# Spacing the recurrence tasks of a hybrid pooling and recurrence block

## The chip, the cores and the metric

The kernel runs on one core of a Trainium2 chip. The metric is the device time of one execution in microseconds (us); the kernel before takes 2507.37 us in the median of three runs (2506.67 to 2508.52).

## The reference

One layer on a sequence of 2048 positions with 1024 channels, all in float32:

- `xn = rmsnorm(x)`; one input projection `z = xn @ w_in` gives pooling channels, and for a gated recurrence of 4 heads of width 128 the queries `q`, forget logits `f`, values and output gate; also two branch gates of 1024 channels.
- Branch A: trailing-window means (windows 2, 4, 8, 16, one for each group of 128 channels) minus the token, a small matrix for each group, then `w_pa`.
- Branch B: for each head a state `S` of 128 x 128, `S_t = diag(f_t) S_(t-1) + (1 - f_t) v_t`, output `q_t S_t`, normalized, gated, then `w_pb`.
- The branches are merged with the gates, projected with `w_o` and added to `x`.
- Then a feed-forward block: up-projection to 2 x 2816, a causal convolution of width 3, a gated product, down-projection, and a last normalization.

## The kernel before, in words

TensorE does all matrix products. Each weight and each activation is split into a high and a low part, and a product is three matmuls for each 128 rows of depth. The large products use a scheme with seven block products in place of eight (P1 to P7), with the sums and differences of blocks made beforehand by VectorE, ScalarE, Pool and DMAs.

The sequence is worked in two halves of 1024 positions. Each half goes through `mixer` and then `ffn`. A mixer first computes values and output gate (`io`) and stores them in memory (`vd`, `zd`). It then runs 14 **units** in the order of the table `PROJ` (L55): `fq` h is the projection for head h, `g` the branch gates, `u` the pooling channels. A unit is seven products of 12 matmuls, for both blocks of 512 positions of the half. In the first mixer a unit also makes sums of weights and stores them for the second, and eight units are each followed by a small product of weights (`both`, L967, tiles `cw`). After the units come the products `pa` (branch A), `pb` (branch B) and `wo`.

Side work runs as Python generators (**tasks**) that are advanced while the instructions are written down: every 6 main matmuls (`MM_PER_TICK`, L79) there is a **tick**, and a task that yields n goes on n ticks later. So ticks set where a side instruction stands in its engine's queue among the main ones. Each engine works through its queue in order.

- `hgrn_task` (L996) is the recurrence of one head for one block of 512 positions: loads of values (L1002), then levels of doubling width, each with small matmuls into `pl` (L1059, L1105, L1118), masked copies into `at` on VectorE (L1073, L1112, L1125) and multiplications of `q`, `k` and `f`; then the transpose `pk` (L1139), the product `pv` with the values (L1148), the state chain `ss` on VectorE (L1156), the output `po` (L1164, L1166), its gating `ot` (L1177) and the transpose back `pt` (L1183). The task of a head's second block waits, before `pv`, until the first block's has written its `po`.
- When an `fq` unit ends, two such tasks (both blocks of one head) are put in `queue` (L1454). Three runners (L1426, L1434) each take one when they are free.
- `pool_task` (L944) makes the window sums of one group, on Pool for even groups and on VectorE for odd ones, from the results of a `u` unit; the second `u` unit has groups 2 and 3. The result is spilled to memory (`md`).
- `pa_task` (L1498) starts in the last unit: it loads the pooled blocks (`mx`) on SyncE's queue and makes the forms that `pa` multiplies. `o_task` (L1636) loads the heads' results and splits them from place 17 on (`O_PLACE`, L70; a place is one product of the last unit or of `pa`).

SyncE issues most loads in one queue: weights (`raw`), `v`, `z`, `mx`. All 512-wide work tiles come from one pool of 77 (`N_SLOTS`, L60), and the eight PSUM banks from another.

Of the kernel before, what the change touches and what calls it, by code (L numbers as in the profile page):

```python
# [51 lines left out]
FORM = {"P1": "B11", "P2": "B21", "P3": "B22", "P4": "T4", "P5": "T1", "P6": "T2", "P7": "T3"}  # L52
FIRST = ("P1", "P6", "P5")
BANK = {"P1": "X", "P2": "X", "P6": "Z", "P7": "Z", "P4": "Z", "P5": "V", "P3": "V"}
PROJ = (("fq", 0), ("g", 0), ("u", 0), ("fq", 1), ("g", 1), ("g", 2), ("fq", 2), ("g", 3),  # L55
        ("u", 1), ("g", 4), ("fq", 3), ("g", 5), ("g", 6), ("g", 7))

M_ORDER = (0, 4, 1, 5, 2, 6, 3, 7)

# [7 lines left out]
GO_IO = (("P2", 1), ("P2", 0))  # L67
G_POOL = 4
CW_AT = 2
O_PLACE = 17  # L70
FIN_WAIT = 4
AHEAD = 3
# [6 lines left out]
MM_PER_TICK = 6  # L79
# [3 lines left out]
def tile_trunk(  # L83
# [26 lines left out]
    def slot(name, cols=TB, dt=F32):  # L110
        return slots.tile([P, cols], dt, tag="s", name=name, padded_shape=[P, 528])

    def bank(name, cols=512):
        return banks.tile([P, cols], F32, tag="b", name=name, padded_shape=[P, 512])
# [6 lines left out]
    count = [0, None]  # L121
# [167 lines left out]
    def in_turn(ins):  # L289

        tc.add_manual_dep(ins.ins, count[1].ins.name, mybir.DependencyInfo(
            mybir.DependencyClass.NoSync, mybir.DependencyReason.SCHED_ONLY), reason="in turn")
        return ins
# [72 lines left out]
    def plan_io(b0):  # L366
        sevens = {}
        for p in IO_ORDER:
            for k in range(4):

                q = [w_io[k, :, c * 512 : (c + 1) * 512] for c in (0, 3, 1, 2)]
                one = {"P1": 0, "P2": 1, "P4": 3}
                if p in one:
                    plan_one("io", q[one[p]])
                    continue
                if b0:
                    plan_one("io", lambda k=k, p=p: kept["io", k, p])
                    continue
                if p == "P5":
                    if not k:  # L380
                        for i in range(4):
                            r0, r2 = (w_io[i, :, c * 512 : (c + 1) * 512] for c in (0, 1))
                            sevens[i] = stream.raw(r2, r0)
                    plan_one("io", lambda k=k: kept.get(("io", k, "P5")))
                    continue
                if p == "P6":
                    raws = [stream.raw(q[i]) for i in (2, 3, 0)]
                elif p == "P7":
                    raws = [sevens[k]]
                else:  # L390
                    raws = [stream.raw(lambda k=k: kept.get(("io", k, "P6")), q[1])]

                def fn(nm, k=k, p=p, raws=raws):
                    if p != "P6":
                        keep(("io", k, p), raws[0].tile, True)
                        return raws[0].tile
                    t = raws[0].tile
                    for i, r in enumerate(raws[1:]):
                        t2 = slot(f"{nm}s{i}")
                        dve.tensor_tensor(t2, t, r.tile, ALU.add)  # L400
                        t = t2
                        keep(("io", k, "P6" if i else "P5"), t)
                    return t

                stream.op("io", fn, raws)

    def plan_unit(key, src, kind, i, order, b0):
        mv, mg = proj_tiles(kind, i)
        if b0:
            unit = sums_of_unit(src, mv, mg, lambda p: lambda: kept["in", (kind, i), SUM_OF[p]])  # L410
        else:
            unit = weights_of_unit(quarters(src[mv], src[mg]), (kind, i))
        for p in order:
            fn, raws = unit[p]()
            stream.op(key, fn, raws)

    def plan_mixer(b0):
        plan_io(b0)
        for n, (kind, i) in enumerate(PROJ):
            if not b0 and (kind, i) == ("u", 0):  # L420
                r = stream.raw(pool_wt)
                stream.op("pw", None, [r])
            plan_unit("in", w_in_t, kind, i, ORDER, b0)
            if not b0 and 0 <= n - CW_AT < 8:
                g, c = divmod(n - CW_AT, 2)
                r = stream.raw(w_pa[g][:, c * 512 : c * 512 + 512])
# [569 lines left out]
    def hgrn_task(b, h, d, q, vd, zd, od):  # L996
        def head_of(src, key):
            t = slot(f"{key}{b}_{h}")
            sp.dma_start(t.rearrange("p (c v) -> p c v", c=NT), src[:, :, h * P : (h + 1) * P])
            return t  # L1000

        vt = head_of(vd, "v")  # L1002
        ks = slot(f"k{b}_{h}")
        act.activation(d, d, AF.Identity, bias=lbt[:, 2, h : h + 1], scale=lbt[:, 3, h : h + 1])
        act.activation(ks, d, AF.Identity, bias=1.0, scale=-1.0)
# [14 lines left out]
        def mask(key, n):  # L1020
            m = masks[key]
            return m.unsqueeze(1).to_broadcast([P, n, m.shape[1], m.shape[2]])
# [67 lines left out]
        for lv in (0, 1, 2, 4, 6):  # L1090
            hh = 1 << lv
            if lv in (2, 4):
                yield from two_levels(hh)
                continue
            nb = P // (2 * hh)
            qv = q.rearrange("p (c b t h) -> p c b t h", c=NT, t=2, h=hh)
            av = att.rearrange("p (c b t h) -> p c b t h", c=NT, t=2, h=hh)
            if lv < 2:
                qd, ad = ((q1, ae), (q2, ao))[lv]
                if lv == 1:  # L1100
                    act.copy(q2[:, :, 0].rearrange("p c (b h) -> p c b h", h=2), qv[:, :, :, 1, :])
                    yield AHEAD
                pa_ = bank(f"pl{b}_{h}_{hh}")
                for c in range(NT):
                    ins = pe.matmul(pa_[:, c * P : (c + 1) * P], ks[:, c * P : (c + 1) * P],  # L1105
                                    qd[:, c].rearrange("p s x -> p (s x)"),
                                    start=True, stop=True)
                    if not c:
                        in_turn(ins)
                yield 2  # L1110
                pv4 = pa_.rearrange("p (c s x) -> p c s x", c=NT, s=2)
                dve.copy_predicated(ad, masks[-1 - lv].to_broadcast([P, NT, 64]), pv4[:, :, 1])  # L1112
                pv4 = pv4[:, :, 0].rearrange("p c (b h) -> p c b h", h=hh)
            else:
                yield AHEAD
                pa_ = bank(f"pl{b}_{h}_{hh}", 256)
                for c in range(NT):
                    ins = pe.matmul(pa_[:hh, c * hh : (c + 1) * hh], ks[:, c * P : c * P + hh],  # L1118
                                    qv[:, c, 0, 1, :], start=True, stop=True)
                    if not c:  # L1120
                        in_turn(ins)
                yield 2
                act.copy(av[:hh, :, 0, 1, :], pa_[:hh].rearrange("p (c h) -> p c h", c=NT))
            if lv < 2:
                dve.copy_predicated(av[:, :, :, 1, :], mask(hh, NT), pv4)  # L1125
            q3 = q.rearrange("p (b t h) -> p b t h", t=2, h=hh)
            k3 = ks.rearrange("p (b t h) -> p b t h", t=2, h=hh)
            d3 = d.rearrange("p (b t h) -> p b t h", t=2, h=hh)
            full = [P, NT * nb, hh]
            if lv:  # L1130
                dve.tensor_tensor(q3[:, :, 1, :], q3[:, :, 1, :],
                                  d3[:, :, 0, 0:1].to_broadcast(full), ALU.mult)
            dve.tensor_tensor(k3[:, :, 0, :], k3[:, :, 0, :],
                              d3[:, :, 1, 0:1].to_broadcast(full), ALU.mult)
            dve.tensor_tensor(d3[:, :, 0, 0:1], d3[:, :, 0, 0:1], d3[:, :, 1, 0:1], ALU.mult)
        yield 4
        pk = bank(f"pk{b}_{h}")
        for c in range(NT):
# [270 lines left out]
    def mixer(b0, forms, late):  # L1409
        vd = [dram.tile([P, NT, 512], F32, tag=f"vd{b0}_{hf}", name=f"vd{b0}_{hf}")  # L1410
              for hf in range(2)]
# [9 lines left out]


        queue = []
        taken = [0]

        def runner():  # L1426
            while taken[0] < 2 * HEADS:
                if queue:
                    taken[0] += 1
                    yield from hgrn_task(*queue.pop(0))  # L1430
                else:
                    yield 1

        runners = [Task(runner()) for _ in range(N_RUN)]  # L1434
        fq = {}
# [121 lines left out]
        oT = {}  # L1557
        for n, (kind, i) in enumerate(PROJ):
            if not b0 and (kind, i) == ("u", 0):
                held["w"] = stream.get("pw")  # L1560
            u = Unit(f"{kind[0]}r{b0}_{i}", "in", emits[kind](i))
            for p in ORDER:
                u.multiply(p, forms, late)
                u.after(p)
                if n == len(PROJ) - 1:
                    if p == "P1":
                        quiet[0] = True
                        mtask = Task(pa_task())
                    place[0] += 1
            if not b0 and 0 <= n - CW_AT < 8:  # L1570
                both(n - CW_AT, held["w"])
                if n - CW_AT == 7:
                    stream.used(1)
# [62 lines left out]
        def o_task():  # L1636
            t = {}
            for hf in range(2):
                for g in range(HEADS):
                    while (b0 + hf, g) not in od:  # L1640
                        yield 1
                    t[hf, g] = fetch(od[b0 + hf, g], f"oT{b0 + hf}_{g}")
            while place[0] < O_PLACE:
                yield 1
# [363 lines left out]
```

## Time and profile before

| | us |
|---|---|
| median of three runs | 2507.37 |
| profiled execution, device time | 2510.01 |
| its span, first to last instruction | 2508.3 |
| TensorE busy | 2480.1 |
| VectorE busy | 2010.1 |
| ScalarE busy | 1200.3 |
| Pool busy | 816.2 |

A busy TensorE isn't always TensorE at its peak, since the ends of matmuls are modelled. PE in the rows is TensorE, PEld its weight load, DVE is VectorE, ACT ScalarE, POOL Pool, SP SyncE; a q behind a name is that engine's own queue. `L1073` is line 1073 of the kernel before.

### The profile page before, as it was taken

Reading aid. Unit: us, or ns where it says so; the run is one execution under the profiler, and the core shown is the slowest. Engines: PE = TensorE matmul, PEld = TensorE weight load, DVE = VectorE, ACT = ScalarE, POOL = GpSimd, SP = SyncE. Lnnn points to the kernel's source line nnn. Section 1 sums busy time; section 2 is a strip of 40 time slices with the busy share of each in tenths; the row PEclk is TensorE's granted clock in tenths of the full one; section 3 lists DMA queues with packets and bytes.
Section 4 is the critical chain, followed back from the end, with each engine's and each line's share of the span. In section 5 each row is a group of like instructions: output and inputs, shape, how many; then the busy total and the mean of one; then the engine's idle time right before and its main releaser. Section 6 shows DMA issues by size and latency. Waiting matters only on the chain.

```text
span 2508.3 us, 36750 instructions
## 1 busy us (share of the span) xinstructions
PE 2480.1 (99%) x11940; PEld 2014.5 (80%) x11940; DVE 2010.1 (80%) x3606; ACT 1200.3 (48%) x2264; POOL 816.2 (33%) x1139
## 2 busy tenths in 40 slices
PE   9999999999999999999999999999999999999998
PEld 7877877788888888888888888887888888888887
DVE  7789778988899778885586887689979988778755
ACT  6524433435545545554465344443355555445534
POOL 4344353502344334461240212223033433325410
PEclk9999999999999999999999999999999999999999
DMA  8878878587898879997344343447443444447852
GB/s 271 277 191 238 245 216 232 204 250 246 201 251 236 224 233 244 264 362 250 132 148 153 114 135 110 143 147 247 141 151 122 154 149 139 150 135 244 323 165 100
DMA packets 257696, 497.75 MB, mean 198 GB/s; under 512 B 26912, under 2 KB 47520, under 8 KB 257184
## 3 DMA queue, kind: packets, MB, share of 16 engines
q1 hardware_dynamic: 189872, 317.53, 38.5%
q0 software_dynamic: 42656, 112.74, 17.6%
q10 hardware_dynamic: 24976, 65.13, 7.5%
q8 instruction: 94, 1.54, 0.2%
q14 instruction: 98, 0.80, 0.1%
HBM read 383.63 MB, written 189.27 MB: 228 GB/s over the span
## 4 chain that ended last, share of the span: by engine, by line
PE 88%; DVE 6%; DMA 2%; issue 1%; POOL 1%; ACT 1%; SPq 0%; ACTq 0%; DVEq 0%; POOLq 0%
PE dn_P L149 16%; PE up_Z L149 15%; PE up_V L149 10%; PE up_X L149 10%; PE wo_P L149 6%; PE gr_Z L149 4%; PE pb L149 4%; PE io_Z L149 3%; PE gr_V L149 3%; PE gr_X L149 2%; PE fr_Z L149 2%; PE io_V L149 2%; PE fr_V L149 1%; PE fr_X L149 1%; DVE at L1073 1%
## 5 line engine op out<-in xcount | busy, mean ns | idle before, releaser
L245 ACT CAST ops<-raw 128x512 fp32r<-128x512 f32 x792 | 488.5, 620 | 816.2 <-PE dn_P L149 181.4
L246 DVE TENSOR_TENSOR ops<-raw,ops 128x512 fp32r<-128x512 f32 x792 | 590.6, 749 | 198.0 <-ACT ops L245 192.3
L1742 DVE SCALAR_TENSOR_TENSOR e<-h,cols,e 128x512 f32<-128x512 f32 x176 | 143.2, 818 | 30.5 <-ACT e L1740 23.5
L1740 ACT ACTIVATE e<-h,cols 128x512 f32<-128x512 f32 x176 | 142.2, 814 | 25.2 <-DVE h L1198 18.4
L992 POOL DMA_DIRECT2D g_P<-dg_P x154 | 83.7, 545 | 162.3 <-PE dn_P L149 115.0
L1745 DVE SCALAR_TENSOR_TENSOR e<-h,cols,e 128x512 f32<-128x512 f32 x176 | 133.8, 770 | 2.5
L1311 POOL TENSOR_TENSOR gf_P<-e,e 128x512 f32<-128x512 f32 x44 | 61.2, 1393 | 149.9 <-DVE e L1751 96.0
L467 POOL TENSOR_TENSOR raw<-raw,raw 128x512 f32<-128x512 f32 x36 | 48.6, 1351 | 171.1 <-DVE ops L246 143.7
L1311 POOL TENSOR_TENSOR gf_P<-gf_P,e 128x512 f32<-128x512 f32 x44 | 59.1, 1344 | 71.7 <-DVE e L1751 71.2
L1735 POOL COPY h<-h 128x2 f32<-128x2 f32 x88 | 40.9, 476 | 116.6 <-DVE h L1197 107.0
L1749 ACT ACTIVATE e<-e 128x512 f32<-128x512 f32 x88 | 55.6, 632 | 37.8 <-DVE e L1745 37.2
L1073 DVE COPY_PREDICATED at<-m,pl 32x64 f32<-32x64 uint8 (+1 forms) x288 | 68.6, 248 | 6.3
L1737 POOL COPY hist<-h 128x2 f32<-128x2 f32 x88 | 35.4, 402 | 117.0 <-DVE h L1198 115.2
L1484 ACT ACTIVATE gt<-gt,cols 128x512 f32<-128x512 f32 x48 | 34.8, 725 | 69.8 <-DVE gt L1198 51.4
L1198 DVE TENSOR_TENSOR h<-up_u,up_V 128x512 f32<-128x512 f32 x88 | 60.0, 682 | 10.1 <-PE up_V L149 9.7
L1042 POOL COPY qm<-q 128x64 f32<-128x64 f32 x64 | 32.7, 538 | 93.6 <-DVE q L1048 30.0
L1286 DVE TENSOR_TENSOR x<-x,wo_P 128x512 f32<-128x512 f32 x88 | 55.9, 680 | 6.3 <-PE wo_P L149 5.9
L1286 DVE TENSOR_TENSOR ac<-ac,dn_P 128x512 f32<-128x512 f32 x72 | 47.0, 680 | 16.2 <-PE dn_P L149 15.8
L1451 POOL TENSOR_TENSOR q<-q,qs 128x512 f32<-128x512 f32 x16 | 21.7, 1357 | 115.3 <-ACT qs L1450 115.2
L1236 ACT COPY up_e<-up_X 128x512 f32<-128x512 f32 x44 | 25.8, 587 | 59.8 <-PE up_X L149 54.8
L1735 POOL COPY h<-hist 128x2 f32<-128x2 f32 x88 | 44.8, 516 | 28.5 <-DVE m_T42l L681 28.5
L1765 POOL DMA_DIRECT2D dg_P<-gf_P x88 | 50.7, 576 | 8.1 <-POOL gf_P L1311 7.4
(1334 smaller groups left out, 8020.3 us busy)
## 6 DMA issues: line engine op xcount, KB each, us to landing
g_P<-dg_P POOLq DMA_DIRECT2D x154, 256.0 KB, 5.9
raw<-in_w_up_t SPq DMA_DIRECT2D x132, 256.0 KB, 3.1
raw<-in_w_in_t SPq DMA_DIRECT2D x98, 256.0 KB, 3.6
dg_P<-gf_P POOLq DMA_DIRECT2D x88, 256.0 KB, 3.8
dg_P<-e SPq DMA_DIRECT2D x66, 256.0 KB, 3.6
raw<-in_w_dn SPq DMA_DIRECT2D x66, 256.0 KB, 3.7
x<-in_x SPq DMA_DIRECT2D x64, 256.0 KB, 5.1
gd<-gt ACTq DMA_DIRECT2D x64, 256.0 KB, 2.6
```

The source lines that it names most:

```text
L149: count[1] = pe.matmul(*args, **kw)
L245: self.mark = act.copy(hi, v)
L246: low = self.low = dve.tensor_tensor(lo, v, f32(hi), ALU.subtract)
L992: eng.dma_start(t, d)
L1073: dve.copy_predicated(to, m, ps[r, :, s].rearrange("p c (b h) -> p c b h", h=k))
L1198: return dve.tensor_tensor(dst, t, ps, ALU.add if how == "add" else ALU.subtract)
L1286: dve.tensor_tensor(t, t, ps[j], ALU.add if sg > 0 else ALU.subtract)
L1311: pin(eng.tensor_tensor(t, x0, x1, op))
L1735: pool.tensor_copy(h[:, 0:2], hist[:, mt] if hf == 0 else hs[s, 0][:, TB : TB + 2])
L1740: in_turn(act.activation(t, h[:, 2:], AF.Identity, bias=col(o_cb + mt), scale=col(o_cw + 4 * MF + mt)))
L1742: in_turn(second(dve.scalar_tensor_tensor(t, h[:, 1 : 1 + TB], col(o_cw + 2 * MF + mt), t, ALU.mult, ALU.add)))
L1745: dve.scalar_tensor_tensor(t, h[:, 0:TB], col(o_cw + mt), t, ALU.mult, ALU.add)
```

## The change

Four edits, all on where instructions stand in the queues:

- A runner takes a task only if at least 20 ticks have gone by since the last task was taken. The counter of ticks is that of the main matmuls.
- In `PROJ` the unit `("fq", 3)` moves from place 11 to place 10, and `("u", 1)`, with the second pooling, from place 9 to place 11; `("g", 4)` moves from 10 to 9.
- The load of the values in a task is written down after the last level, ahead of the `yield 4` before `pk`, in place of the task's start.
- The constant `TASK_GAP` is new.

```diff
-PROJ = (("fq", 0), ("g", 0), ("u", 0), ("fq", 1), ("g", 1), ("g", 2), ("fq", 2), ("g", 3),
-        ("u", 1), ("g", 4), ("fq", 3), ("g", 5), ("g", 6), ("g", 7))
+PROJ = (("fq", 0), ("g", 0), ("u", 0), ("fq", 1), ("g", 1), ("g", 2), ("fq", 2), ("g", 3), ("g", 4), ("fq", 3), ("u", 1), ("g", 5), ("g", 6), ("g", 7))
...
+TASK_GAP = 20
...
-        vt = head_of(vd, "v")
         ks = slot(f"k{b}_{h}")
...
             dve.tensor_tensor(d3[:, :, 0, 0:1], d3[:, :, 0, 0:1], d3[:, :, 1, 0:1], ALU.mult)
+        vt = head_of(vd, "v")
         yield 4
         pk = bank(f"pk{b}_{h}")
...
-        taken = [0]
+        taken = [0, -TASK_GAP]
 
         def runner():
             while taken[0] < 2 * HEADS:
-                if queue:
+                now = count[0] // MM_PER_TICK
+                if queue and now - taken[1] >= TASK_GAP:
                     taken[0] += 1
+                    taken[1] = now
                     yield from hgrn_task(*queue.pop(0))
                 else:
                     yield 1
```

## The prediction

> **What bounds the kernel now.** I read the head of the page first, then its chain.
>
> ```profile
> span 2508.3 us, 36750 instructions
> PE 2480.1 (99%) x11940; PEld 2014.5 (80%) x11940; DVE 2010.1 (80%) x3606; ACT 1200.3 (48%) x2264; POOL 816.2 (33%) x1139
> PE 88%; DVE 6%; DMA 2%; issue 1%; POOL 1%; ACT 1%; SPq 0%; ACTq 0%; DVEq 0%; POOLq 0%
> ```
>
> TensorE is the bound: it idles only 2508.3 - 2480.1 = 28.2 us. The change adds and removes no arithmetic, so it can only return time in which TensorE waits or runs slowly. The profiled execution took 2510.01 us, 1.7 more than its span and 2.6 more than the 2507.37 median; I take differences from the profile and apply them to the median.
>
> Where is that time? I asked for busy time by stretch. Two long ones come first: from the first matmul of the projections to the first of `pa`, in the first and in the second mixer. They compute the same for different rows. Then single units (`fq3` done to `g5` done, and so on), first mixer beside second.
>
> ```profile
> 98.30:454.20 355.90, 345.95 (x2018) 278.89 (x2017) 284.11 (x707) 149.96 (x339) 149.85 (x159) 0.99 0.79 229
> 1354.10:1688.20 334.10, 333.61 (x2002) 273.33 (x2001) 263.97 (x698) 145.32 (x327) 70.56 (x93) 1.00 0.42 133
> 373.10:398.80 25.70, 24.60 (x182) 20.03 (x180) 23.77 (x54) 13.25 (x28) 11.48 (x13) 1.00 1.03 265
> 398.80:429.30 30.50, 27.00 (x143) 20.99 (x141) 26.61 (x84) 9.99 (x21) 9.64 (x10) 0.89 0.70 198
> 1615.30:1639.20 23.90, 23.90 (x181) 19.91 (x179) 21.57 (x58) 12.43 (x26) 5.70 (x11) 1.00 0.37 120
> 1639.20:1663.40 24.20, 24.02 (x152) 18.79 (x142) 22.42 (x78) 8.63 (x18) 0.00 (x0) 1.00 0.36 112
> 1569.70:1595.00 25.30, 25.30 (x138) 21.53 (x137) 15.24 (x31) 9.39 (x28) 11.00 (x14) 1.00 0.40 125
> 301.60:326.70 25.10, 24.40 (x147) 18.93 (x143) 23.98 (x77) 7.90 (x17) 8.93 (x10) 1.00 0.64 213
> 167.80:197.00 29.20, 26.37 (x137) 21.55 (x135) 19.18 (x35) 8.42 (x27) 13.14 (x15) 1.00 0.91 230
> ...
> L149 PE MATMUL cw<-raw,ops 128*128 128x512 f32 x16 | 8.4, 605 | 0.0
> ```
>
> The columns are length, then busy time of PE, PEld, DVE, ACT, POOL, then clock, DMA share, GB/s. The first mixer is 355.9 - 334.1 = 21.8 us longer. It has one kind of TensorE work that the second lacks, the 16 `cw` matmuls of 8.4 us (last row). The other **13.4 us are lost**: 9.95 as plain idle (355.90 - 345.95), the rest as slower running. The second mixer idles 0.49 us. So the prize lies in the first mixer, and in the `pa` stage behind each:
>
> ```profile
> PE pa_Z L149 <- DVE pa_u L1238: 4.3, 4, 1.8
> PE pl L1118 <- DVE at L1073: 4.0, 3, 3.0
> PE po L1166 <- DVE ss L1156: 1.9, 2, 1.6
> PE pl L1105 <- ACT q L1014: 1.1, 2, 0.6
> PE fr_Z L149 <- DVE fr_u L1242: 1.0, 1, 1.0
> ```
>
> These are TensorE's waits, in total, count and longest; four of the five end on VectorE.
>
> **How the change moves things.** Product and tick:
>
> ```profile
> 101.27 2.77 PE fr_Z L149 x12
> ```
>
> Twelve matmuls of a product take 2.77 us, so a tick (6) is 1.39 us and a unit 14 ticks of main work. Adding the yields of a recurrence task gives 43 ticks, and its VectorE work, all levels, falls in the first 23. Before, the tasks start at ticks 14, 14, 56, 57, 98, 99, 154, 154: each pair runs its heavy part together, then its light part together. VectorE shows this in the rows above: 21.57, then 22.42 of 24.2 with the pair's levels, but 15.24 of 25.3 in the unit of a pair's light half. After, `fq3` is the tenth unit (ends at tick 140) and tasks start at 14, 34, 56, 76, 98, 118, 140, 160. Twenty ticks is close to 23, so heavy parts follow one another and a light part lies beside each. The last task ends at tick 203 instead of 197; its result is split only from place 17, tick 196 + 10 x 2 = 216, so 13 ticks (18 us) cover it. Without that cover the delay would be 6 x 1.39 = 8.3 us in each mixer.
>
> **a. The wait at the last pair's levels.**
>
> ```profile
> 413.02 0.68 PE L1118 MATMUL pl<-q,k 128*64 128x64 f32 x8
> 413.74 5.70 DVE L1073 COPY_PREDICATED at<-m,pl 32x64 f32<-32x64 uint8 x22
> 418.49 1.09 PE L1118 MATMUL pl<-q,k 128*64 128x64 f32 x8 [2.95 <-DVE at L1073]
> ...
> 418.40:424.80 6.40, 6.31 (x21) 5.12 (x22) 6.13 (x18) 2.07 (x4) 0.00 (x0) 0.51 0.91 185
> 425.50:431.00 5.50, 5.50 (x30) 4.55 (x29) 2.72 (x4) 3.66 (x6) 1.29 (x1) 1.00 0.55 188
> ```
>
> Both tasks' 24 masked copies stand in VectorE's queue at once, and the second task's `pl` matmuls, with all main matmuls behind them on TensorE, wait 2.95 us. Right after, the granted clock is 0.51 for 6.40 us, which costs 6.40 x 0.49 = 3.1 us. With one task at a time there are 12 copies, half the burst, 12 x 5.70/22 = 3.1 us. The wait then mostly lies behind the main products. Bounds 0 and 2.95 + 3.1; I take all **6.1**, since the same place in the second mixer (24.02 busy of 24.20) shows that the work fits.
>
> [...]
>
> **b. The pair's state updates.**
>
> ```profile
> 181.00 0.39 PE L149 MATMUL fr_Z<-x_T33l,ops 128*128 128x512 f32 x1
> 182.96 0.49 PE L1166 MATMUL po<-ss,q 128*128 128x128 f32 x2 [1.57 <-DVE ss L1156]
> ```
>
> The second task's `pv` needs the first one's state, so in a pair both state chains are interleaved. 20 ticks apart they aren't. Bounds 0 and 1.9 (the `po` row of the waits); I take **1.9**.
>
> **c. The rest of the first mixer.** 13.4 - 6.1 - 1.9 = 5.4 us of small VectorE lateness, such as units 373.10 (25.70 against 23.90). Bounds 0 and 5.4. Half of it is tied to DMA and Pool, which the second mixer has less of (share 0.79 against 0.42, Pool 149.85 against 70.56) and which stay. I take **2.7**.
>
> **d. The `pa` stage.** Two tails of tasks (`ot` and the split forms) meet VectorE there; one remains. Bounds 0 and 4.3; I take half, **2.1**.
>
> **e. What is paid.** A switch between the two kinds of matmul costs little:
>
> ```profile
> 160.34 0.47 PE L149 MATMUL ur_Z<-x_T40h,ops 128*128 128x512 f32 x1
> 160.64 0.39 PE L149 MATMUL ur_Z<-x_T40l,ops 128*128 128x512 f32 x1
> 160.88 0.39 PE L149 MATMUL ur_Z<-x_T40h,ops 128*128 128x512 f32 x1
> ```
>
> The first step after the small matmuls is 0.30 us, the next 0.24. Pairs that shared a burst no longer do; three more bursts a mixer cost 6 x 0.06 = **0.4**.
>
> The second pooling now runs at ticks 150 to 178 instead of 122 to 150. Before, a pair's light half lay beside it (15.24 of 25.3 with the pooling in it). After, it meets tasks 7 and 8 in their levels. Bounds: the nearest units with VectorE that full are 301.60, idle 0.70 us, and 167.80, the first pooling, 29.20 - 26.37 = 2.83 us. I take two units of 0.7, in both mixers less in the second: **2**. Its results are due at tick 184, 6 ticks after its end.
>
> The values' load moves from a task's start to 8 ticks before `pv`. It frees one of 77 tiles for some 28 ticks; waits for a tile show in the first pooling:
>
> ```profile
> DVE p L961 <- DMA md<-p: 5.0, 1, 5.0
> DVE fr_u L1242 <- DMA md<-p: 3.7, 1, 3.7
> ...
> 166.42 1.03 PE L1139 MATMUL pk<-ident,k 128*128 128x128 f32 x8
> 173.46 1.05 PE L1148 MATMUL pv<-v,kt 128*128 128x128 f32 x8
> ...
> L999 SPq DMA_DIRECT2D z<-zd x16: 529/530/1322, 176.8 to 1672.9; - x16
> ...
> DMA to landing us min/median/max: 2.1/3.9/14.3
> ```
>
> From `pk` to `pv` is 4 ticks and 7.0 us, so 8 ticks are 14 us. SyncE's queue runs late: the load of `z` stands ahead of `pv` in the code but was issued 176.8 - 173.5 = 3.3 us behind it. That leaves 10.7 us; the landing of `v` took 3.9 in the median (last row), 14.3 at worst. Bounds 0 and 3.6 a task; I take **0**, with the medians. Queued behind a late `v` on TensorE would be every main matmul.
>
> **Sum:** 6.1 + 1.9 + 2.7 + 2.1 - 0.4 - 2 = 10.4, rounded to 10: 2507.4 - 10 = **2497.4 us**.
>
> **Rivals.** *Everything goes* (0.10): all 13.4 and the 4.3, nothing paid: 2489.7. For it: the second mixer runs such work with 0.49 idle.
>
> *The stall moves to the second pooling* (0.20). What VectorE beside Pool looks like:
>
> ```profile
> 170.04 3.78 DVE L956 TENSOR_TENSOR s<-u 128x526 f32<-128x526 f32 x1
> 176.24 0.68 DVE L956 TENSOR_TENSOR s<-s 128x512 f32<-128x512 f32 x1
> ...
> 170.33 1.80 POOL L467 TENSOR_TENSOR raw<-w52s,raw 128x512 f32<-128x512 f32 x1
> 171.72 1.52 POOL L956 TENSOR_TENSOR s<-u 128x512 f32<-128x512 f32 x1
> ```
>
> An add of 0.68 took 3.78 while Pool added. The level steps of tasks 7 and 8 would be stretched so too, as six Pool adds now fall beside them; twice 3.1 us in the first mixer, with one gap of 2.95 and its clock loss of 3.1 there, leave 10.4 - 6.1 = 4 of gain at most, less the second mixer's share of 1: 2504. Against: only one add in view is stretched so far. [...]
>
> *The waits come from late transfers, so spacing does nothing* (0.15): the first mixer's extra 13.4 would stay with its DMA share of 0.79; only b and half of d remain, less e: 1.9 + 1 - 2.4, about 2507.
>
> *Values late* (0.10), the slower side: three of the first mixer's eight loads land after 14.3 us. Each holds TensorE 3.6 us and loses the clock for 3.1: 3 x 6.7 = 20 against 10 of gain, 2517. It decides from 10.7 us of landing on. Against: the median is 3.9.
>
> **Chances.** Forecast 0.45, own range 2492 to 2502. About 0.2% (5 us) can be told from no change here. Faster: forecast and the first rival, a little of the second, 0.58; same: the second and third mostly, 0.30; slower 0.12. The range 2488 to 2509 reaches over the first three rivals and leaves out the late values.
>
> **What would show it.** After: no wait of `pl` for `at` near 3 us, and no stretch with a clock near 0.5 in the first mixer; first mixer near 346 us; VectorE's busy time flat from unit to unit; few waits of `po` on `ss`. Wrong: TensorE waiting at `pv` with a DMA as releaser, a new gap in the units beside the second pooling, or a first mixer still near 355.

## The result, and the profile after

The changed kernel takes 2522.14 us in the median of four runs against 2507.72: a ratio of 1.0058, 95% interval 1.0041 to 1.0076. It is 14.4 us **slower**; the prediction was 2497.4, faster by 10. The head of its page:

```profile
span 2520.3 us, 36678 instructions
PE 2489.4 (99%) x11940; PEld 2018.4 (80%) x11940; DVE 2019.0 (80%) x3606; ACT 1203.8 (48%) x2264; POOL 797.7 (32%) x1139
```

TensorE idles 30.9 us in place of 28.2, and its busy time grew by 9.3 us with the same 11940 matmuls, so most of the loss shows as longer busy time. A lower clock is part of it: read in steps of 1 us, it costs 3.4 us in the first mixer before (one stretch, from 417 us on) and 6.8 after (from 177, 395 and 453 us on; it reads 0.50 in each), and nothing in the second mixer. The rest of the longer busy time is not assigned. TensorE's waits after:

```profile
PE gr_Z L149 <- DVE gr_u L1242: 7.8, 5, 2.2
PE pa_Z L149 <- DVE pa_u L1238: 4.7, 4, 2.5
...
PE fr_Z L149 <- DVE fr_u L1242: 2.1, 1, 2.1
PE pk L1139 <- DVE k L1132: 2.0, 1, 2.0
PE fr_Z L149 <- DVE fr_u L1238: 1.7, 1, 1.7
```

The waits of `pl` for `at` and of `po` for `ss` are gone, as predicted. In their place stand waits for `gr_u` and `fr_u`, the evacuations on VectorE that empty PSUM bank Z for the next product. Before, `fr_u` cost 1.0 us in all and `gr_u` 0.7. By stretch, with the same columns as in the prediction: both mixers' units, the unit of the first pooling (`fq1`), the two units after the second pooling's (`g5`, `g6`), and the stage of `pa` and `pb` in both mixers:

```profile
98.50:459.50 361.00, 349.01 (x2012) 280.09 (x2011) 290.06 (x705) 150.13 (x331) 146.22 (x158) 0.98 0.79 226
1360.20:1698.10 337.90, 335.61 (x1996) 272.74 (x1995) 267.41 (x696) 145.14 (x319) 58.06 (x91) 1.00 0.41 130
162.90:195.30 32.40, 28.58 (x177) 22.34 (x175) 22.52 (x67) 8.54 (x24) 15.04 (x14) 0.95 0.68 163
375.60:405.40 29.80, 26.43 (x125) 20.23 (x124) 25.85 (x59) 8.41 (x17) 16.76 (x18) 0.89 0.74 172
405.40:433.20 27.80, 25.79 (x173) 20.82 (x171) 25.66 (x72) 10.74 (x27) 9.87 (x12) 1.00 0.77 223
459.50:547.50 88.00, 85.16 (x375) 68.86 (x374) 77.39 (x115) 29.22 (x57) 26.07 (x19) 1.00 0.71 236
1698.10:1785.50 87.40, 85.50 (x376) 68.89 (x375) 80.79 (x121) 29.16 (x58) 27.03 (x19) 1.00 0.69 243
```

The last two stretches before, for comparison:

```profile
454.20:541.10 86.90, 84.75 (x370) 68.24 (x369) 78.16 (x114) 28.14 (x50) 27.13 (x18) 1.00 0.73 243
1688.20:1775.00 86.80, 84.66 (x370) 68.28 (x368) 81.18 (x119) 28.01 (x50) 25.93 (x17) 1.00 0.70 239
```

The units lose 361.0 - 355.9 = 5.1 and 337.9 - 334.1 = 3.8 us, `pa` with `pb` 1.1 and 0.6. That is 10.6 of the 12.0 by which the spans differ. The clearest place is the first pooling (32.4 us against 29.2). The two units beside the second take 57.6 us against 25.7 + 30.5 = 56.2, where term a alone had promised a gain of 6.1. In the second mixer the loss is spread over many units.

What a stop looks like there, in the timelines of TensorE and VectorE after:

```profile
395.31 0.92 PE L1139 MATMUL pk<-ident,k 128*128 128x128 f32 x4 [1.99 <-DVE k L1132]
397.60 0.80 PE L149 MATMUL gr_Z<-x_T40h,ops 128*128 128x512 f32 x1 [1.38 <-DVE gr_u L1242]
398.19 0.63 PE L149 MATMUL gr_Z<-x_T40l,ops 128*128 128x512 f32 x1
398.62 0.63 PE L149 MATMUL gr_Z<-x_T40h,ops 128*128 128x512 f32 x1
...
391.35 0.56 DVE L1072 COPY_PREDICATED at<-m,pl 32x64 f32<-32x64 uint8 x2
391.82 0.41 DVE L1134 TENSOR_TENSOR f<-f 128x256 f32<-128x256 f32 x1
...
395.08 1.03 DVE L1134 TENSOR_TENSOR f<-f 128x4 f32<-128x4 f32 x1
396.12 0.70 DVE L956 TENSOR_TENSOR s<-s 128x524 f32<-128x524 f32 x1
396.86 0.69 DVE L1242 TENSOR_TENSOR gr_u<-gr_Z,gr_e 128x512 f32<-128x512 f32 x1
...
394.76 1.32 POOL L956 TENSOR_TENSOR s<-s 128x524 f32<-128x524 f32 x1 [3.73 <-DMA od<-oh]
```

From 391 on VectorE has the masked copies of task 7 (L1072), the first steps of task 8 (L1134 at 391.82 and others) and an add of the pooling (L956) in one queue, and `gr_u`, for which all of TensorE waits, stands behind them. The last step of task 7 ahead of it, on 128 x 4 elements, takes 1.03 us while an add of the pooling runs on Pool (last row). And the granted clock is 0.50 from 396 to 402 us: from 398.19 to 398.62 is 0.43 us, where from 390.88 to 391.11 it was 0.23, and the unit's mean clock is 0.89.

### The profile page after: what moved, and what is told of

It reads as the page before. It is cut to its first block, busy times and chain, and to the rows that moved or that the text cites. A ratio compares the mean times of both kernels' runs of the same rounds, so it can differ in the third digit from the quotient of the medians.

```text
span 2520.3 us, 36678 instructions
## 1 busy us (share of the span) xinstructions
PE 2489.4 (99%) x11940; PEld 2018.4 (80%) x11940; DVE 2019.0 (80%) x3606; ACT 1203.8 (48%) x2264; POOL 797.7 (32%) x1139
## 3 DMA queue, kind: packets, MB, share of 16 engines
q8 instruction: 94, 1.54, 0.2%
## 4 chain that ended last, share of the span: by engine, by line
PE 88%; DVE 6%; DMA 2%; issue 1%; ACT 1%; POOL 1%; SPq 0%; ACTq 0%; DVEq 0%; POOLq 0%
PE dn_P L149 16%; PE up_Z L149 15%; PE up_X L149 10%; PE up_V L149 10%; PE wo_P L149 5%; PE gr_Z L149 4%; PE pb L149 4%; PE io_Z L149 3%; PE gr_V L149 3%; PE gr_X L149 2%; PE fr_Z L149 2%; PE io_V L149 2%; PE fr_V L149 2%; PE fr_X L149 2%; PE ur_Z L149 1%
## 5 line engine op out<-in xcount | busy, mean ns | idle before, releaser
L1744 DVE SCALAR_TENSOR_TENSOR e<-h,cols,e 128x512 f32<-128x512 f32 x176 | 142.5, 814 | 30.5 <-ACT e L1742 23.9
L1742 ACT ACTIVATE e<-h,cols 128x512 f32<-128x512 f32 x176 | 142.5, 816 | 25.3 <-DVE h L1198 18.3
L1072 DVE COPY_PREDICATED at<-m,pl 32x64 f32<-32x64 uint8 (+1 forms) x288 | 71.4, 248 | 22.0 <-PE pl L1058 16.5
L1041 POOL COPY qm<-q 128x64 f32<-128x64 f32 x64 | 23.1, 379 | 128.1 <-DVE q L1081 34.4
```

The lines of the kernel that those rows point to most:

```text
L1072: dve.copy_predicated(to, m, ps[r, :, s].rearrange("p c (b h) -> p c b h", h=k))
L1742: in_turn(act.activation(t, h[:, 2:], AF.Identity, bias=col(o_cb + mt), scale=col(o_cw + 4 * MF + mt)))
L1744: in_turn(second(dve.scalar_tensor_tensor(t, h[:, 1 : 1 + TB], col(o_cw + 2 * MF + mt), t, ALU.mult, ALU.add)))
```

## Experiments

The theories: **A**, the second pooling, which had a stretch without levels (the heavy part of a task) beside it, now lies on the levels of the last two tasks; **B**, the spacing itself costs, since levels are then always in progress and the first pooling has no free stretch either; **C**, the late values; **D**, added after the first four runs, a last task that ends late falls on `pa`'s own VectorE work. Ratios are to the kernel before on the same chip, with 95% intervals.

### One part at a time

`gap_only`: the spacing alone, with the old `PROJ` and the values loaded at the task's start.

```diff
+TASK_GAP = 20
...
-                if queue:
+                if queue and now - taken[1] >= TASK_GAP:
```

> Only the spacing of 20 ticks, old order of units, values loaded early. The last task now starts at tick 174 and ends at 217, one tick behind the place where its result is split (216). Theory A (the second pooling now lies on the levels of tasks 7 and 8): without the move of the pooling no loss in the units, so about 2505 to 2512, and a wait before pb of a few us. Theory B (the spacing itself costs: with a task's levels always in progress VectorE has no slack left for any pooling, the first one included): 2515 to 2525. Theory C (the late load of the values): about the time before or below.

Measured: 2528.15 us, 1.0079 (1.0064 to 1.0094).

`gap_late`: spacing and late values, old `PROJ`.

> Spacing and late values, old order of units. Theory A: 2503 to 2511. Theory B: 2513 to 2525, with the first pooling's units (some 165 to 195 us) as slow as in the changed kernel. Theory C: like the changed kernel, 2520 or so, with waits of pv on a DMA.

Measured: 2529.23 us, 1.0085 (1.0070 to 1.0100).

`order_only`: the new `PROJ` alone (`TASK_GAP = 0`, values early).

> Only the order of units, no spacing, values early. Tasks 7 and 8 start together at tick 140 and the second pooling runs beside their levels. Theory A: 2511 to 2520, with TensorE waiting in the two units beside the second pooling. Theory B: within 3 of the time before, 2505 to 2511, since a light half still follows. Theory C: no change, 2507.

Measured: 2524.93 us, 1.0067 (1.0050 to 1.0084).

`late_v_only`:

```diff
-        vt = head_of(vd, "v")
         ks = slot(f"k{b}_{h}")
...
+        vt = head_of(vd, "v")
         yield 4
         pk = bank(f"pk{b}_{h}")
```

> Only the late load of the values. Theory A and theory B: no loss, 2504 to 2509 (a tile is free for longer). Theory C: 2512 to 2522, with waits of pv on a DMA.

Measured: 2502.91 us, 0.9980 (0.9970 to 0.9989).

C falls: late values alone are a gain of 5 us. Spacing alone costs 20 us and the order alone 17, each more than the whole change and, like `gap_late`, above every range expected of them, so they share a cause or repair each other. Spacing with the new order but early values wasn't tried. In `gap_late` the units of both mixers, then `pa` with `pb`:

```profile
100.10:455.20 355.10, 343.93 (x1990) 277.18 (x1988) 285.16 (x686) 147.91 (x329) 143.62 (x157) 0.99 0.80 227
1367.20:1698.90 331.70, 331.70 (x1973) 270.60 (x1972) 262.24 (x676) 143.77 (x317) 58.45 (x91) 1.00 0.42 130
455.20:553.70 98.50, 92.48 (x398) 73.00 (x397) 82.30 (x132) 30.53 (x61) 28.16 (x20) 0.97 0.68 219
1698.90:1796.20 97.30, 91.28 (x397) 72.20 (x396) 86.11 (x138) 30.40 (x61) 26.95 (x19) 0.98 0.65 222
...
PE pv L1149 <- DMA v<-vd: 3.5, 1, 3.5
```

In the old order the units lose nothing in sum (355.1 and 331.7 against 355.9 and 334.1, with some 28 matmuls now behind them); `pa` and `pb` lose 11.6 and 10.5, and the last task ends at tick 217, in the midst of them. So the new order had a use: it bought that back and lost elsewhere. The last row is the prediction's late value, once, 3.5 us.

In `order_only` most of the loss is in one unit of each mixer, `g5`, beside the second pooling (first two rows, against 25.7 and 23.9 before). TensorE waits 6.22 us there for a `gr_u` that stands behind an add of the pooling and the levels of two tasks (some of VectorE's rows below):

```profile
376.60:409.80 33.20, 25.68 (x148) 20.10 (x142) 28.82 (x86) 6.80 (x15) 16.75 (x18) 0.90 0.52 135
1621.30:1654.50 33.20, 27.19 (x175) 20.32 (x170) 27.75 (x87) 7.58 (x16) 10.55 (x13) 0.90 0.25 73
...
394.46 0.79 PE L149 MATMUL gr_Z<-x_T30h,ops 128*128 128x512 f32 x1 [6.22 <-DVE gr_u L1238]
...
388.38 1.22 DVE L956 TENSOR_TENSOR s<-u 128x526 f32<-128x526 f32 x1
...
390.57 1.47 DVE L1086 TENSOR_TENSOR k<-k,f 128x384 f32<-128x384 f32 x1
391.96 1.23 DVE L1088 TENSOR_TENSOR f<-f 128x8 f32<-128x8 f32 x1
```

The second mixer shows it too, with a DMA share of 0.25, and in neither mixer does VectorE wait for a transfer ahead of this stop: it isn't DMA.

### Where the pooling stands, and where the last task ends

`pool_back` keeps spacing and late values:

```diff
-... ("g", 3), ("g", 4), ("fq", 3), ("u", 1), ("g", 5), ...
+... ("g", 3), ("u", 1), ("fq", 3), ("g", 4), ("g", 5), ...
```

> The changed kernel with the second pooling unit put back to place 9, the last head's unit still one place sooner (place 10), the gates' unit behind both. Theory A (the second pooling on the levels of the last two tasks): the waits behind it go, 2503 to 2512. Theory B (the spacing itself): 2515 to 2525, the loss stays. Theory D (a last task that ends late, on top of pa's own VectorE work): partly better, 2510 to 2518, with the pa stage as long as in the changed kernel.

Measured: 2521.70 us, 1.0058 (1.0043 to 1.0073). A as written missed; the time lies in B's range.

`head_sooner` is the same order without spacing.

> As the run before, but without spacing: pairs start together, values late. Theory A: no loss, since the pooling is away from the levels, 2500 to 2507, near the run with only the late values (2502.9). Theory that the sooner head by itself costs: 2512 to 2525, as with the whole new order (2524.9).

Measured: 2520.95 us, 1.0055 (1.0040 to 1.0070). A missed as well; the time lies in the range of the other theory, that the sooner head costs by itself. VectorE and TensorE in `pool_back`, in the unit after `fq3`:

```profile
363.49 0.43 DVE L1130 TENSOR_TENSOR q<-q,f 128x256 f32<-128x256 f32 x1 [1.54 <-ACT q L1100]
...
366.51 1.75 DVE L961 SCALAR_TENSOR_TENSOR p<-s,u 128x512 f32<-128x512 f32 x1
...
375.02 0.69 DVE L961 SCALAR_TENSOR_TENSOR p<-s,u 128x512 f32<-128x512 f32 x1 [5.15 <-DMA md<-p]
...
369.93 0.79 PE L149 MATMUL gr_Z<-x_T30h,ops 128*128 128x512 f32 x1 [6.68 <-DVE gr_u L1238]
```

The pooling is still in progress at 366 and 375, after `fq3` ended at 352.6: it ends at tick 126 + 24 = 150, and the levels start at 140. One place isn't enough. Only the old order without spacing leaves two units, ticks 126 to 154, between `u1` and the next levels. That the pooling is the cause in these two runs is read from the timeline and wasn't tested by taking it away. VectorE itself waits 1.54 us for ScalarE just ahead of the stop of 6.68 us (first row) and 5.15 us for a store just behind it, so late copies of `q` and the sooner head by itself stay rivals here.

`last_pair_together`: old order, late values, spacing for seven tasks.

```diff
-if queue and now - taken[1] >= TASK_GAP:
+if queue and (now - taken[1] >= TASK_GAP or taken[0] == 2 * HEADS - 1):
```

> Old order of units, late values, spacing of 20 ticks for seven tasks, the eighth starts at once with the seventh. Theory D: the 10 us that pa and pb lost with spacing and the old order (97 against 87 us) come back in both mixers, 2502 to 2510. Theory B: some 5 to 10 us stay lost in the units, 2512 to 2520.

Measured: 2515.95 us, 1.0039 (1.0024 to 1.0053). `pa` and `pb` are back at 85.6 and 86.9 us, so D holds for them, while 8 us stay lost: the first mixer's units take 360.5 us, the first pooling's alone 34.0 against 29.2.

### Taking the pooling away

`after_no_sums` leaves out the window sums of groups 2 and 3 in the changed kernel (the adds are eight on VectorE and six on Pool a mixer).

```diff
-        while k < w:
+        while k < w and g < 2:
```

> The changed kernel with the window sums of the second pooling left out (groups 2 and 3 only: their doubling adds, 14 on VectorE and 10 on Pool a mixer or fewer; the rest of their path stays). Theory A: the loss in the units beside it goes, 2505 to 2513. Theory B and D: nearly no change, 2518 to 2523.

Measured: 2510.72 us, 1.0010 (1.0001 to 1.0019). A holds: 11.4 us less than the changed kernel.

`narrow_second` keeps these adds and their tiles but gives them 16 columns, and makes `p` from `u`, which leaves out the same sums:

```diff
+            if g >= 2:
+                add.tensor_tensor(t[:, 16:32], s[:, 16:32], s[:, 16:32], ALU.add)
+            else:
+                add.tensor_tensor(t[:, a:528], s[:, a:528], s[:, a - k : 528 - k], ALU.add)
...
+        dve.scalar_tensor_tensor(p, (u if g >= 2 else s)[:, 16:528], 1.0 / w, u[:, 16:528], ALU.mult, ALU.subtract)
```

> The changed kernel; the window adds of the second pooling keep their number, order and tiles, but work on 16 columns in place of some 520 (its result then comes from the unsummed input). So demand for tiles stays, the time on VectorE and Pool goes. Theory A1 (the adds' time on VectorE and Pool is what stops TensorE): like the run without the sums (2510.7), 2508 to 2514. Theory A2 (the adds' tiles are what is lacking): 2517 to 2523.

Measured: 2512.85 us, 1.0021 (1.0010 to 1.0032), near the run without them. So it is the adds' time, or what hangs on it, and not their number. A short add also gives its tiles back sooner, so the run alone does not rule tiles out; but beside the second pooling of the changed kernel's first mixer VectorE waits 0.7 us in all for transfers. VectorE's time and Pool's weren't told apart.

`narrow_both` does this to the first pooling too, `narrow_both_before` to the kernel before, and `narrow_both_late` to the kernel with only the late values; all three leave out the window sums.

> As the run before, with the adds of the first pooling narrowed too. If the spaced tasks lose at the first pooling for the same reason (A1), the unit of some 162 to 195 us in the first mixer falls from 32 to 29 us and the whole by 3 to 5 more: 2504 to 2510. If that loss is tiles waiting for slow stores (A2 there), it stays as the run before within 2.

Measured: 2507.87 us, 0.9998 (0.9989 to 1.0008).

> The kernel before with the adds of both poolings narrowed in the same way, as the baseline of the two runs above. Theory A: before, the poolings lay beside the light halves of pairs and cost nearly nothing, so 2503 to 2508. If they cost as much there, 2495 to 2500, and the collision would not tell the two kernels apart.

Measured: 2504.90 us, 0.9987 (0.9978 to 0.9996).

> The kernel before with the late load of the values and both poolings' adds narrowed to 16 columns. If the gain of the late values is their own, 2498 to 2501, and spacing and order then cost some 8 us beside the poolings. If that gain came from the tiles that the poolings want, narrowing has taken it already: 2503 to 2506, and only 3 us are left.

Measured: 2504.47 us, 0.9987 (0.9977 to 0.9996). The units of the first mixer and its first pooling in `narrow_both`, then the units of the first mixer in `narrow_both_before`:

```profile
98.00:448.70 350.70, 343.97 (x2011) 277.13 (x2010) 279.54 (x708) 150.37 (x331) 132.22 (x158) 1.00 0.81 233
162.40:188.80 26.40, 26.40 (x176) 21.15 (x174) 21.89 (x72) 9.76 (x25) 11.03 (x14) 1.00 0.89 234
```

```profile
98.20:449.10 350.90, 343.35 (x2018) 277.96 (x2017) 277.15 (x707) 150.26 (x339) 140.79 (x159) 1.00 0.81 233
```

The first pooling's unit falls from 32.4 to 26.4 us, without any idling, and the two kernels' first mixers are equal. More than one execution shows that loss: this unit takes 30.7 to 34.6 us in all seven kernels with 20 ticks and the full first pooling, and 28.3 to 29.2 in the four whose pairs start together.

Whether the first pooling loses by the adds' time or by tiles is not told apart. In the changed kernel VectorE waits there for two stores (rows below, the 4.9 us just ahead of a stop of TensorE); with `narrow_second` these waits are 5.2 and 1.7 us, with `narrow_both` they are gone. But the kernel before waits 5.0 and 3.7 us there too, so these waits alone don't make the difference.

```profile
DVE p L961 <- DMA wb<-cw: 4.9, 1, 4.9
DVE s L956 <- DMA md<-p: 1.9, 1, 1.9
```

With late values in both, spacing and order cost 2522.1 - 2502.9 = 19.2 us with full poolings and 2507.9 - 2504.5 = 3.4 with narrow ones. **The poolings carry some 16 of 19 us.** What is shown is that the poolings' adds and the moved tasks collide: narrow adds are worth 14.3 us in the changed kernel and 3 in the one before.

The waits do not all go with them. `narrow_both` still waits 7.2 us for `gr_u` at L1245 in all (7.8 with the full adds, at L1242). In `g5`:

```profile
368.90:395.40 26.50, 23.64 (x125) 18.51 (x124) 21.47 (x59) 8.91 (x18) 9.15 (x14) 1.00 0.82 194
...
389.77 0.50 PE L149 MATMUL gr_Z<-x_T40h,ops 128*128 128x512 f32 x1 [2.86 <-DVE gr_u L1245]
...
388.75 0.17 DVE L957 TENSOR_TENSOR s<-s 128x16 f32<-128x16 f32 x1 [3.46 <-POOL s L957]
388.84 0.16 DVE L1137 TENSOR_TENSOR f<-f 128x4 f32<-128x4 f32 x1
...
388.50 0.21 POOL L957 TENSOR_TENSOR s<-s 128x16 f32<-128x16 f32 x1 [7.88 <-DMA od<-oh]
```

Here VectorE isn't full: it waits 3.46 us for an add on Pool, which had waited 7.88 us for a store of `oh`, and `gr_u` stands behind. The stop is about as long as the two in the changed kernel (1.99 + 1.38), but the clock stays at 1.00, and the unit takes 26.5 us in place of 29.8. So in this pair of profiles the clock makes nearly all of the unit's gain; how much of the medians' gain it makes isn't shown. The late values' gain is gone as well when the poolings are narrow (2504.5 against 2504.9), so it too seems to hang on them. Tiles are the likely link but not a shown one: `p` still waits 5.0 us for the store of another `p` with late values.

### Other spacings

All with the old order, and 4, 8 or 12 ticks; `gap4_only` has early values, the others late ones.

```diff
-TASK_GAP = 20
+TASK_GAP = 4
```

> Old order of units, late values, spacing of 4 ticks in place of 20: a pair's bursts no longer fall together, but its light half still follows and the pooling has its free stretch; the last task ends at tick 201, well before 216. If lockstep bursts cost what the prediction said (terms a, b), 2494 to 2501, below the run with late values alone (2502.9). If any spacing costs, 2505 to 2515.

Measured: 2499.82 us, 0.9970 (0.9960 to 0.9980).

> The run with 4 ticks and late values once more for its interval: 2497 to 2503, and a ratio to the kernel before whose interval lies below 1.

Measured: 2498.71 us, 0.9965 (0.9952 to 0.9979).

> Old order, values early, spacing of 4 ticks. If spacing and values add up (values alone gave -5.1, both -8.3): 2503 to 2506. If the gain of the run with both came from the values alone: 2507 to 2510. If spacing needs the freed tiles: 2510 or more.

Measured: 2505.15 us, 0.9987 (0.9978 to 0.9996).

> Old order, late values, spacing of 8 ticks. A pair's second task ends its levels at tick 14 + 8 + 23 = 45, seven ticks into the first pooling (38). If the loss grows with the overlap of levels and pooling: 2500 to 2505. If only bursts matter: 2496 to 2500.

Measured: 2515.94 us, 1.0042 (1.0025 to 1.0058).

> As before with 12 ticks: the levels of the second task reach tick 49, and the last task ends at 209, seven ticks ahead of 216. By the overlap: 2503 to 2512, slower than with 4 and 8. If only bursts matter: 2496 to 2500.

Measured: 2506.87 us, 1.0000 (0.9990 to 1.0009). Four ticks with late values beat both kernels. Eight ticks miss every expectation, and 12 are better than 8: it isn't one rising curve. With 12 ticks the units take 346.4 and 331.9 us, less than before by 9.5 and 2.2 (with some 25 matmuls fewer in them), but `pa` with `pb` 90.8 and 89.1; with 8 ticks these took 92.4 and 93.4, with one wait of 4.4 or 4.5 us for `pa_u` on VectorE in each mixer. So the last run spaces only the last pair less:

```diff
-                if queue and now - taken[1] >= TASK_GAP:
+                if queue and now - taken[1] >= (4 if taken[0] == 2 * HEADS - 1 else TASK_GAP):
```

> Old order, late values, 12 ticks between tasks but 4 between the last head's two, so the last task ends at tick 201 in place of 209. If the late end is what pa and pb paid for: pa and pb back at 86 to 88 us each (from 90.8 and 89.1), the units at 346 to 349 and 332, and a time of 2495 to 2500. If the length of pa and pb has another cause: they stay near 90, 2502 to 2508.

Measured: 2505.83 us, 0.9991 (0.9982 to 1.0000). Units of the first mixer, `pa` with `pb` twice, and the first pooling's unit, first of `gap12_then4`, then of `gap12_late`:

```profile
98.60:452.90 354.30, 345.04 (x2017) 278.68 (x2016) 285.32 (x703) 149.73 (x339) 146.92 (x159) 0.99 0.80 229
452.90:539.60 86.70, 84.71 (x369) 68.34 (x369) 78.75 (x118) 28.54 (x51) 28.55 (x19) 1.00 0.75 247
1685.40:1771.80 86.40, 84.62 (x370) 68.25 (x369) 81.06 (x122) 28.01 (x50) 27.03 (x18) 1.00 0.72 243
164.90:195.20 30.30, 27.07 (x139) 21.57 (x138) 23.90 (x60) 9.77 (x25) 13.45 (x15) 0.94 0.89 226
```

```profile
98.30:444.70 346.40, 341.42 (x1994) 274.76 (x1993) 278.61 (x696) 147.62 (x329) 144.69 (x157) 1.00 0.81 233
164.60:191.40 26.80, 25.73 (x140) 20.42 (x138) 21.88 (x57) 8.24 (x21) 12.37 (x13) 1.00 0.85 205
```

`pa` and `pb` came back as expected, the time did not: the units grew by 7.9 us. Part is work that returned to them, and 3.5 us are the first pooling, where both kernels have the same instructions in the same order on TensorE, VectorE and Pool. Why 8 ticks are worse than 12, in `pa` and in the first mixer's units (352.0 us against 346.4), is open.

## Why the prediction was wrong

- **The bound** was right: TensorE. What moved were its waits, its slow stretches and some busy time that is not assigned.
- **How the change moves things** was right as far as it went. VectorE did become flatter, and a light half stands beside each heavy one; but two units of the second mixer, beside the poolings, now fill VectorE to 24.5 of 25.5 us and 24.6 of 25.6. The step that failed is the use of this. The row "15.24 of 25.3" was read as slack that spreading would even out; it was the stretch that the pooling lived in, and spreading filled it.
- **Term a** (6.1 us): the wait of `pl` went, as said, but the clock loss didn't go with it: the clock fell after three other waits (1.71, 1.99 and 2.22 us), and the loss in the first mixer doubled, from 3.4 to 6.8 us.
- **Term b** (1.9 us) holds: no wait of `po` for `ss` is left.
- **Term c** (2.7 us) isn't there: the first mixer's units got longer, by 5.1 us. With 4 ticks and late values the units of both mixers do get shorter: 347.6 and 332.0 us in one execution and 350.8 and 332.0 in another, in place of 355.9 and 334.1.
- **Term d** (2.1 us): nothing. The waits of `pa_Z` are 4.7 us in place of 4.3.
- **Term e** is where the sum broke. The second pooling was priced at 2 us from units that VectorE fills to 24 of 25; the runs without or with narrow sums give 9 to 11 (of which at most some 3 are what these adds cost before as well). The first pooling had no term at all, although the spaced tasks lie on it in the same way; narrowing it gave another 5.0 (2512.9 to 2507.9).
- **Late values**: taken as 0 with a slower rival beside it; alone they gave 5.1 us, for a reason that isn't settled. In the profiles some 1.6 us of it are the clock, which fell for a shorter time behind the same wait (last section). That rival's wait showed once each in two runs with the old order (3.5 us in `gap_late`, 2.8 in `last_pair_together`), and not in the changed kernel.
- **The rival that came true** is the second one, the stall that moves to the second pooling. It was given 0.20 and a price that left a gain of 3, since it counted two waits and let the wins of a and b stand. Its place was right and its size too small; its mechanism, level steps that take longer beside Pool's adds, shows as a part of it. In the changed kernel's `g5` three groups of level steps (L1045 x2, L1083, L1134) beside Pool's pooling adds take 1.35, 1.03 and 1.03 us. The first two take 0.47 and 0.15 in `g6` of the same execution (from 421.70 us on, with Pool idle), the third 0.16 in `narrow_both` (the row at 388.84): 2.6 us less in all. No run here separates Pool's whole share.
- Open: the last 3.4 us of spacing and order with narrow poolings (the wait of 2.86 us for Pool and a store is one candidate), and what of the loss is VectorE's time, Pool's or tiles.

## What to carry over

A stretch in which a busy engine has little to do is not free until it is known what else leans on it: list, for each side task, which stretch it runs in, before loads are evened out. Price a queue by what stands behind its longest run of instructions (here the evacuation that frees a PSUM bank), not by its mean load. Try a small shift first: 4 ticks and a later load gained 0.3% (0.9970 and 0.9965 in two runs) where 20 ticks lost.

## What was not expected of the hardware

The clock fell after shorter waits than the one of 2.95 us that the prediction had priced with a clock loss. In the changed kernel's unit `g5` the mean clock was 0.89: it fell from 1.00 to 0.50 at about 395.5 us, after the wait of 1.99 us and before that of 1.38. In `fq1` it was 0.95, with a fall at about 177.1 us after a wait of 1.71, and at about 453.5 us it fell after one of 2.22; after waits of 2.08 and 2.54 us, which ended at 188.4 and 471.6 us, it stayed at 1.00. In the kernel before it fell at about 417.9 us, inside the wait of 2.95 that ended at 418.49. Nor did the length of a wait settle the loss. Behind the same wait of `pl` (2.95 us in the kernel before, 3.0 with late values alone) the unit's mean clock was 0.89 of 30.5 us before and 0.94 of 29.3 with late values (row below), a loss of 3.4 and 1.8 us, and behind the 2.86 us in `narrow_both` it was 1.00. So in these profiles waits of 1.7 to 3.0 us came with a clock loss between nothing and 3.4 us, and a price for such a wait has to allow for both.

```profile
397.40:426.70 29.30, 25.59 (x151) 19.78 (x141) 26.40 (x85) 9.97 (x21) 9.69 (x10) 0.94 0.77 216
```

And one and the same order of instructions took 26.8 us in one execution and 30.3 in another at the first pooling (`gap12_late` and `gap12_then4`, clocks 1.00 and 0.94), so that a stage of a single profile is known there to some 3.5 us only.
